# Mixing the dilated groups' outputs on POOL during the next heads' attention, loading the last projection's weights inside the gates, and splitting the norms over two engines

## The chip, the cores and the metric

The program runs on one core of a Trainium2 chip. The metric is the device time of one execution in microseconds (us); times of several runs are given with their median. The engines are called as in the profile: PE (matrix products), DVE (vector), ACT (scalar), POOL (GpSimd) and SP (SyncE, which here issues every DMA, the transposing ones too).

## The reference

A trunk of two layers on 2048 tokens of width 1024. The second layer is the one that the change touches most.

```python
def dilated_mixer(h, w_in):
...
    for g, (window, dil) in enumerate(DIL_GROUPS):      # (128, 1), (512, 4), (2048, 16)
...
        o, lse = dilated_group(q, k, qkv[:, :, 2], window, dil)
        outs.append(o)
        lses.append(lse)
    wts = jax.nn.softmax(jnp.stack(lses, axis=0), axis=0)
    o = jnp.einsum('gbth,gbthd->bthd', wts, jnp.stack(outs, axis=0).astype(jnp.float32))
...
def reference(x, mem, mem_norm_w, norm_w, w_memkv, w_out, w_in_a, ...):
    mem_n = rmsnorm(mem, mem_norm_w)
    for i in range(DEPTH):
        h = rmsnorm(x, norm_w[i])
...
        mem_o = memory_attention(q_mem, mem_n, w_memkv[i])
        branch = jnp.concatenate([mix, mem_o], axis=-1) * jax.nn.silu(gate)
        x = x + branch @ w_out[i]
    return rmsnorm(x, final_norm_w)
```

Layer 0 mixes with gated linear attention (GLA), layer 1 with windowed attention in three groups (six heads of 128 each per group), whose outputs are added with softmax weights. Each layer has four heads of attention into 256 memory tokens (the last 256 of the 1024 branch columns), a SiLU gate and an output projection.

## The kernel before, in words

Tokens go in 16 blocks of 128 or 4 chunks of 512. Products that need more than half precision are made of two half-precision parts and three matmuls (`mm3`, L174-177). The instructions are written in the order of the Python text, and a scheduler then reorders them within each engine by a simulation of its own, keeping dependencies; each engine executes its own stream in order, SP's DMA queue too.

The stages, in the order of time:

- **GLA blocks** (the loop at L605): for each block the projections in four parts (`pre_a` to `pre_d`), `gla1` and `gla2`. Into blocks 7 to 14 the loop also puts the column norms of layer 1's input weights: `norm_of` (L345-351, called at L637-639, four per block, 32 in all) loads a 1 MB tile of weights by `load_raw` and sums the squares of its two halves, both on ACT (L351). The norms are needed to scale the weights before they are split into half-precision parts.
- **A2**, memory attention, gate and output projection of layer 0 by blocks, and the seven operand combinations of a Strassen-like product (`h2s`, stored as `h2_d`; L689-806). Memory attention is `mem_qT`, `mem_sc` (L248-269: scores, maximum L260, its scaling L261, exponentials L265, splitting by `split_P` L165-172) and `mem_pv` (L271-292).
- **The passage** into layer 1: the last operands are transposed, stored and loaded again (L812-822), and `load_ws` (L826) loads the first set of weights, which ACT (L838), DVE (L839) and POOL (L842-848) scale and combine.
- **Products and attention**: `products()` (L1226) yields after each of the seven products of a half (`sw_half`, L854). The main loop (L1247-1256) goes through nine units (three pairs of heads, three groups each), for each of two heads through eight blocks; it calls `advance(to)` (L1242) for product pieces, `att_scores` (L1033), one more piece, and the value products of a block before. The probabilities are split into two parts (ACT L168, POOL L169) and transposed by a DMA (L170) into `pt`, which the value products read. The outputs go to `o_d`, the softmax statistics to `st_d`.
- **Gates** (L1271-1311): `gate_prep` (L1137) makes from the statistics of a pair the factors of the three groups and stores them in `f_d`. `gate_half` (L1161) computes a gate by `silu` (DVE L299, ACT L301-303, DVE L307) and hands each 128 x 512 tile to `gate_item` (L1170): for each of three groups it loads factors (`fb`, a row broadcast to 128 partitions) and outputs (`og`), multiplies (POOL L1182 and L1186, DVE L1189), adds (DVE L1191), multiplies by the gate (DVE L1194) and stores to `br_d`. `mem_item` (L1197) does the same for memory attention's output. The loop at L1307 interleaves the stages of layer 1's memory attention, 19 steps of four, with 56 pieces of the gates.
- **Last projection** (L1316-1377): after all gates, four 1 MB loads of `w_out` (L1344), each split into a high part on ACT (L1345) and a low part on DVE (L1346), then 16 blocks: load branch and residual (`load_b`, L1325), split, products, RMSNorm, store.

Of the kernel before, what the change touches and what calls it, by code (L numbers as in the profile page):

```python
# [7 lines left out]
F32 = mybir.dt.float32  # L8
# [26 lines left out]
def trunk(ctx, tc, a, out):  # L35
# [211 lines left out]
    def mem_sc(mem, qmT, wk, tg, hls, wp3=None):  # L247
# [3 lines left out]
        ps = []  # L251
        for hh in range(2):
            s = bank(ps_g)
# [7 lines left out]
            V.tensor_scalar(out=m2, in0=m2, scalar1=nsc, scalar2=LSP, op0=ALU.mult, op1=ALU.add)  # L261
            p_ = tl(wp3 or wk, [P, 512], F32, tg[1 + hh])
            for jj in range(2):
                j = hh * 2 + jj
                A.activation(out=p_[:, jj * 256:(jj + 1) * 256], in_=s[:, jj * 256:(jj + 1) * 256],  # L265
                             func=AF.Exp, scale=sc, bias=m2[:, jj:jj + 1], accum_out=den[:, j:j + 1])
# [4 lines left out]
    def mem_pv(mem, sd, om, po):  # L271
# [16 lines left out]
        V.tensor_scalar(out=den, in0=den, scalar1=ov, scalar2=None, op0=ALU.mult)  # L288
# [31 lines left out]
    st_d = [tl(dram, [2, 3, T], F32, f"std{h}") for h in range(6)]  # L320
    f_d = [tl(dram, [4, 3, 512], F32, f"fd{h}") for h in range(6)]
# [14 lines left out]
    def load_raw(idx, spool):  # L336
        raw = tl(spool, [P, KT, 256], F32, "stg")
# [7 lines left out]
    def norm_of(idx, spool, junkp):  # L345
        raw = load_raw(idx, spool)
        for j in range(2):
            jv = tl(junkp, [P, D], BF16, "e").rearrange("p (k n) -> p k n", k=KT)
            rv = raw[:, :, j * P:(j + 1) * P]
            acc = nrm[:, 2 * idx + j:2 * idx + j + 1]  # L350
            A.activation(out=jv, in_=rv, func=AF.Square, accum_out=acc)  # L351
# [26 lines left out]
    with ExitStack() as c1:  # L378
# [226 lines left out]
        for b in range(NB):  # L605
            S = gla2(b, pres[b][1], aqs[b], S)
            if b + 2 < NB:
                hT = ga(b + 2)
            if b + 2 < NB:
                pres[b + 2] = pre_a(b + 2, hT)  # L610
            if b + 2 < NB:
                pre_b(*pres[b + 2])
            if b + 2 < NB:
                pre_c(*pres[b + 2])
            if b + 2 < NB:
                pre_d(*pres[b + 2])
            if b + 1 < NB:
# [19 lines left out]
            if 7 <= b < 15:  # L637
                for j in range(4):
                    norm_of((b - 7) * 4 + j, (stg, sga)[j % 2], k2)

    ch = ctx.enter_context(ExitStack())
    h2p = ch.enter_context(pool("h2p", 1, "right"))
    wo_p = ch.enter_context(pool("wo", 1, "right"))
# [4 lines left out]
    with ExitStack() as c2:  # L648
# [138 lines left out]
        for j in range(4):  # L787
            wt = tl(wo_p, [P, 2, KT, 256], F16, f"wo{j}")
# [648 lines left out]
```

## Time and profile before

| | us |
|---|---|
| runs, median of 3 (lowest to highest) | 2884.04 (2874.2 to 2885.29) |
| the profiled execution | 2881.88 |
| its span | 2880.0 |
| PE busy (share of the span) | 2524.7 (88%) |
| DVE | 1655.0 (57%) |
| ACT | 1363.5 (47%) |
| POOL | 844.2 (29%) |

The mean granted PE clock is 0.948. A line such as L1191 is a line of the kernel; an arrow in a name goes from the output tile to the inputs. A group's row gives count, busy us, mean ns of one, and the idle time in front of it with what ended it. A row of waits gives engine, line, what was waited for, total us, times and the longest. The stages lie, in us from the span's start: GLA blocks with norms 280 to 440, A2 500 to 955, the passage 955 to 1001, products and attention 1001 to 2335, gates 2335 to 2658, the passage to the last projection 2658 to 2692, the last projection to 2880.

### The profile page before, as it was taken

To read this page: it belongs to the slowest core of one execution; us is meant where nothing else is said; L and a number is where in the kernel's file an instruction comes from. 1 tells how busy PE (TensorE), PEld (TensorE's weight loads), DVE (VectorE), ACT (ScalarE), POOL (GpSimd) and SP (SyncE) were. 2 spreads that over 40 slices of the span, in tenths; PEclk is the share of its full clock that TensorE was granted. 3 is DMA by queue.
4 is the path that set the end of the run, shared out by engine and by line. 5 is a ranking of instruction groups with operands and counts; after the bars stand their busy time and mean duration, and the time that the engine had idled before them with its cause. 6 is when DMAs were issued, how large, how long until landed. Compare 5 with 4: busy or idle time off the path is not lost. (4 is left out here: it accounts for less than half of the span.)

```text
span 2880.0 us, 54886 instructions
## 1 busy us (share of the span) xinstructions
PE 2524.7 (88%) x21264; PEld 1887.1 (66%) x21264; DVE 1655.0 (57%) x3205; ACT 1363.5 (47%) x3033; POOL 844.2 (29%) x709
## 2 busy tenths in 40 slices
PE   7999789999999398999999999999899986665699
PEld 6888679888888364757575747575757743322487
DVE  6445334666666346566656565657465678876433
ACT  6355864644444144555544455545454544542322
POOL 0000000021112134444444444435344445642000
PEclk9999999999999799999999999999999997777799
DMA  6243873466476835677666667666667768987533
GB/s 203 78 137 115 269 218 103 124 138 152 111 156 139 229 114 148 181 168 181 162 167 167 174 162 177 163 167 174 160 165 178 167 170 187 205 190 187 173 133 123
DMA packets 800747, 469.21 MB, mean 163 GB/s; under 512 B 508466, under 2 KB 745700, under 8 KB 799332
## 3 DMA queue, kind: packets, MB, share of 16 engines
q1 hardware_dynamic: 800484, 465.69, 61.7%
q8 instruction: 167, 2.74, 0.4%
q14 instruction: 96, 0.79, 0.1%
HBM read 274.15 MB, written 130.47 MB: 140 GB/s over the span
## 5 line engine op out<-in xcount | busy, mean ns | idle before, releaser
L175 PE MATMUL ps_mm<-w,hT 128*128 128x256 f16 (+1 forms) x1408 | 392.8, 279 | 16.2 <-ACT v L515 7.2
L176 PE MATMUL ps_mm<-w,hT 128*128 128x256 f16 (+1 forms) x1408 | 391.6, 279 | 0.0
L177 PE MATMUL ps_mm<-w,hT 128*128 128x256 f16 (+1 forms) x1408 | 390.7, 279 | 0.4 <-DVE hT L407 0.4
L176 PEld LDWEIGHTS <-w 128*128 128x128 f16 x2032 | 210.7, 104 | 206.4 <-issue 93.4
L839 DVE SCALAR_TENSOR_TENSOR w<-stg,wsc,w 128x512 f16<-128x512 f32 x224 | 209.7, 937 | 189.3 <-ACT w L838 188.0
L177 PEld LDWEIGHTS <-w 128*128 128x128 f16 x2032 | 210.7, 104 | 148.0 <-issue 19.4
L175 PEld LDWEIGHTS <-w 128*128 128x128 f16 x2032 | 210.5, 104 | 131.2 <-issue 16.5
L838 ACT ACTIVATE w<-stg,wsc 128x512 f16<-128x512 f32 x224 | 160.1, 717 | 213.5 <-DMA stg<-in_w_in_b 72.4
L169 POOL TENSOR_TENSOR ph<-pm,ph 128x512 f16<-128x512 f32 (+2 forms) x144 | 144.3, 1003 | 310.0 <-ACT ph L168 226.2
L1076 ACT ACTIVATE pm<-pm,st,qsc 128x256 f32<-128x256 f32 (+1 forms) x288 | 156.9, 545 | 149.5 <-DVE st L1070 148.6
L169 POOL TENSOR_TENSOR stg<-mp,stg 128x512 f16<-128x512 f32 x16 | 18.5, 1157 | 711.3 <-DMA ogd<-og 503.1
L175 PE MATMUL ps_mm<-w,w 128*128 128x128 f16 (+1 forms) x740 | 189.0, 285 | 16.0 <-DVE cx L880 11.5
L945 DVE SCALAR_TENSOR_TENSOR hl<-cx,hl 128x512 f16<-128x512 f32 x162 | 140.8, 870 | 106.3 <-ACT hl L944 105.5
L177 PE MATMUL ps_mm<-w,w 128*128 128x128 f16 (+1 forms) x740 | 188.3, 284 | 0.0
L176 PE MATMUL ps_mm<-w,w 128*128 128x128 f16 (+1 forms) x740 | 188.2, 284 | 0.0
L944 ACT ACTIVATE hl<-cx 128x512 f16<-128x512 f32 x162 | 100.8, 623 | 167.7 <-DVE cx L880 151.7
L176 PEld LDWEIGHTS <-hT 128*128 128x128 f16 x1408 | 140.6, 100 | 38.7 <-issue 18.7
L175 PEld LDWEIGHTS <-hT 128*128 128x128 f16 x1408 | 141.3, 100 | 21.8 <-issue 1.5
L177 PEld LDWEIGHTS <-hT 128*128 128x128 f16 x1408 | 140.6, 100 | 20.1 <-DVE hT L407 0.7
L897 POOL TENSOR_TENSOR u<-u,p 128x512 f32<-128x512 f32 x64 | 90.0, 1406 | 88.3 <-ACT u L875 88.3
L175 PE MATMUL ps_o<-pt,v 128*128 128x128 f16 (+1 forms) x384 | 77.3, 231 | 43.4 <-DMA pt<-ph 42.8
L175 PEld LDWEIGHTS <-h 128*128 128x128 f16 x800 | 88.2, 110 | 39.1 <-issue 36.9
(402 smaller groups left out, 7975.4 us busy)
## 6 DMA issues: line engine op xcount, KB each, us to landing
stg<-in_w_in_b SPq DMA_DIRECT2D x144, 256.0 KB
stg<-in_w_in_b SPq DMA_DIRECT2D x56, 512.0 KB
qkd<-hl SPq DMA_DIRECT2D x144, 192.0 KB
rope<-in_rope SPq DMA_DIRECT2D x36, 512.0 KB
vud<-hl SPq DMA_DIRECT2D x72, 256.0 KB
q<-qkd SPq DMA_DIRECT2D x72, 256.0 KB
od<-osb SPq DMA_DIRECT2D x72, 256.0 KB
og<-od SPq DMA_DIRECT2D x72, 256.0 KB
```

The source lines that it names most:

```text
L169: G.tensor_tensor(out=lo, in0=src, in1=hi, op=ALU.subtract)
L175: PE.matmul(o, sh, mh, start=first, stop=False, skip_group_check=free)
L176: PE.matmul(o, sh, ml, start=False, stop=False, skip_group_check=free)
L177: PE.matmul(o, sl, mh, start=False, stop=last, skip_group_check=free)
L838: A.activation(out=t[:, 0], in_=src, func=AF.Copy, scale=s1)
L839: V.scalar_tensor_tensor(out=t[:, 1], in0=src, scalar=s1, in1=t[:, 0], op0=ALU.mult, op1=ALU.subtract)
L897: G.tensor_tensor(out=u3, in0=u3, in1=p1, op=ALU.add)
L944: A.activation(out=hi, in_=src, func=AF.Copy, scale=SQ)
L945: V.scalar_tensor_tensor(out=lo, in0=src, scalar=SQ, in1=hi, op0=ALU.mult, op1=ALU.subtract)
L1076: A.activation(out=p_, in_=p_, func=AF.Exp, scale=sc, bias=st[:, sj[jj]:sj[jj] + 1], accum_out=st[:, 16 + sj[jj]:17 + sj[jj]])
```

## The change

1. `norm_step` replaces `norm_of`: each call squares the tile that was loaded two calls earlier, in place, one half on ACT and the other on DVE (`tensor_tensor_reduce`), then loads the next. Four calls stand between the parts of each block from block 7.
2. The first weights of layer 1 are loaded in A2's last step, and the second half's operands after the second set's load.
3. `mem_sc` scales the maxima of both halves in one operation. In layer 1 `mem_pv` leaves out the scaling by the values' factor, and `mem_turn`'s copy on ACT takes it over.
4. `gate_item` is gone. `combos` mixes the groups' outputs of a pair of heads: loads as before, multiplications and one addition on POOL, the last multiplication and addition on DVE, and a store to `acc_d`. It is a generator; `tick`, called for each product piece, steps it. Pair 0 runs from unit 3, pair 1 from unit 6, pair 2 from the start of the gates.
5. Between a block's scores and the value products, two product pieces instead of one.
6. `gate_half` loads the mixed output (`oc`), the first step goes to DVE for one tile of four and to POOL for three, the gate times `oc` to POOL.
7. The order of the memory stages in a step, and of the last gate's halves, is another.
8. The last projection's weights are loaded and split by `out_w` between the last pieces of the gates, and so is the first block's `load_b`; the blocks begin with chunk 0. The low parts of the second half are two tiles of 256 columns, so its products with them are two (120 more matmuls).

```diff
+    def norm_step(spool):
+        if spool in raws:
+            idx, raw = raws.pop(spool)
+            acc = nrm[:, 2 * idx:2 * idx + 2]
+            rv = raw[:, :, 0:P]
+            A.activation(out=rv, in_=rv, func=AF.Square, accum_out=acc[:, 0:1])
+            rv = raw[:, :, P:2 * P]
+            V.tensor_tensor_reduce(out=rv, in0=rv, in1=rv, scale=1.0, scalar=0.0, op0=ALU.mult, op1=ALU.add,
+                                   accum_out=acc[:, 1:2])
+        if left:
+            idx = left.pop(0)
+            raws[spool] = idx, load_raw(idx, spool)
...
+            if n == NB - 1:
+                raw0 = load_raw(0, wp, "w")
...
+    def combos(hp, pl, lag):
+        yield from gate_prep(hp, pl)
+        for hf in range(2):
+            for c, i in ((hf, 0), (hf + 2, 1), (hf + 2, 0), (hf, 1)):
+                h = hp * 2 + i
+                acc = None
+                for g in (2, 1, 0):
+                    fb = tl(pl[0], [P, 16, 32], F32, "fb")
...
+                    og = tl(pl[1], [P, 512], F32, "fo")
...
+                    yield lag[0]
+                    if g == 2:
+                        G.tensor_tensor(out=fb, in0=og.rearrange("p (q l) -> p q l", q=16), in1=fb, op=ALU.mult)
+                    elif g == 1:
+                        f1v = fb.rearrange("p (r f) l -> p r f l", f=4)
+                        G.tensor_tensor(out=f1v, in0=og.rearrange("p (f l r) -> p r f l", f=4, r=4), in1=f1v,
+                                        op=ALU.mult)
+                        G.tensor_tensor(out=fb, in0=fb, in1=acc, op=ALU.add)
+                    else:
+                        ov = og.rearrange("p (l q) -> p l q", q=16)
+                        V.tensor_tensor(out=ov, in0=ov, in1=fb.rearrange("p q l -> p l q"), op=ALU.mult)
+                        V.tensor_tensor(out=ov, in0=ov, in1=acc.rearrange("p q l -> p l q"), op=ALU.add)
+                        SY.dma_start(acc_d[h][c], og)
+                    acc = fb
+                    yield lag[1]
...
         def fin(src, ci, ni, ps):
-            sg = tl(gt, [P, 512], F32, "sg")
-            silu(src, 512, [inv], [neg], sg, ge)
-            post(sg, hf + 2 * ci, ni)
+            c = hf + 2 * ci
+            oc = tl(gb, [P, 512], F32, "oc")
+            SY.dma_start(oc, src_of(c, ni))
+            e = tl(ge, [P, 512], F32, "e")
+            (V if ps else G).tensor_scalar(out=e, in0=src, scalar1=neg, scalar2=87.0, op0=ALU.mult, op1=ALU.min)
+            A.activation(out=e, in_=e, func=AF.Exp)
+            A.activation(out=e, in_=e, func=AF.Ln, bias=one1)
+            A.activation(out=e, in_=e, func=AF.Exp, scale=-1.0)
+            G.tensor_tensor(out=e, in0=e, in1=oc, op=ALU.mult)
+            V.scalar_tensor_tensor(out=e, in0=src, scalar=inv, in1=e, op0=ALU.mult, op1=ALU.mult)
+            SY.dma_start(br_d[c][:, :, row + ni, :], e.rearrange("p (n t) -> p n t", n=4))
...
             for n in range(8):
+                if un in (3, 6) and i == 0 and n == 2:
+                    aux[0] = combos(un // 3 - 1, (cf, cg), (2, 1))
                 advance(28 + LEAD + 42 * un + ((42 if un < 8 else 24) * (i * 8 + n)) // 16)
                 att_scores(H, n, pend)
                 if len(pend) > 1:
-                    advance(done[0] + 1)
+                    advance(done[0] + 2)
                     pend.pop(0)()
...
     for t_ in range(19):
-        for k in (3, 2, 1, 0):
+        for n, k in enumerate((1, 3, 0, 2)):
             mem_stage(k, t_ - k)
-            advance((42 * (4 * t_ + 4 - k)) // 76)
+            advance((42 * (4 * t_ + n + 1)) // 76)
+    advance(49)
+    ch.close()
...
+    porder = [0, 1, 2, 3, 8, 9, 10, 11, 4, 5, 6, 7, 12, 13, 14, 15]
+    out_w(0)
+    out_w(1)
+    advance(51)
+    out_w(2)
+    advance(53)
+    out_w(3)
+    nxt = load_b(porder[0], wp)
     advance(10 ** 6)
```

`cf` holds two buffers, `cg` one; in the gates `gb` and `ge` hold three, `gf` two.

How the streams change, at three places. First ACT at the passage into layer 1. Before, behind the last operand combinations (L760, `stg`) come the puts of the first set's weights (L838, `w<-stg`):

```order
L760 ACTIVATE stg_11390<-t_1643_11392 128x512
L760 ACTIVATE stg_11390<-x_11277 128x512
L760 ACTIVATE stg_11390<-x_11144 128x512
L838 ACTIVATE w_11484<-stg_11481,wsc_5437 128x512
L838 ACTIVATE w_11489<-stg_11481,wsc_5437 128x512
L838 ACTIVATE w_11493<-stg_11481,wsc_5437 128x512
```

After, at the same place (the lines are now L778, L853 and L859; `w_11185` is the tile loaded early, `stg_11430` the second set's):

```order
L778 ACTIVATE stg_11322<-t_1586_11324 128x512
L778 ACTIVATE stg_11322<-x_11209 128x512
L778 ACTIVATE stg_11322<-x_11073 128x512
L853 ACTIVATE stg_11430<-stg_11430,wrat_5384 128x8x128
L859 ACTIVATE w_11405<-w_11185,wsc_5382 128x512
L859 ACTIVATE w_11410<-w_11185,wsc_5382 128x512
```

The scaling of the second set's tile has moved ahead of the first set's puts.

Second, SP in a unit of attention. Before, transposes (`pt`), stores and loads of queries, keys and values alternate:

```order
L990 DMA qkd_1_96_184<-hl_20548 192x1x512
L1022 DMA q_20677<-qkd_0_93_181 128x8x128
L1022 DMA k_20678<-qkd_1_94_182 128x8x128
L1025 DMA v_20482<-vud_0_121_209 128x8x128
L1110 DMA od_1_45_133<-osb_20529 128x512
L170 DMA_TRANSPOSE pt_20567<-ph_20566 128x8x128
L990 DMA qkd_0_95_183<-hl_20586 192x1x512
```

After, in a unit with `combos` (L1193 loads factors, L1197 and L1199 a group's outputs, L1212 stores the sum):

```order
L1193 DMA fb_20390<-fd_68_156 128x512
L1212 DMA accd_63_151<-fo_20289 128x512
L170 DMA_TRANSPOSE pt_19965<-ph_19964 128x8x128
L976 DMA vud_1_128_216<-hl_20020 128x1024
L1193 DMA fb_20491<-fd_68_156 128x512
L976 DMA vud_0_127_215<-hl_20074 128x1024
L1199 DMA fo_20392<-od_2_40_128 128x16x32
L976 DMA vud_1_128_216<-hl_20158 128x1024
L170 DMA_TRANSPOSE pt_20104<-ph_20103 128x8x128
```

The transposes now stand behind loads and stores of the combinations, of which `fo` has one buffer.

Third, SP at the end of the gates. Before, the loads of `w_out` (L1344) and of the first block (L1327) stand near and behind the last stores of the gates (`brd`):

```order
L1344 DMA raw_4463_32243<-in_w_out 128x8x256
L1352 DMA fw_32253<-in_final_norm_w 128x1024
L1201 DMA brd_150_238<-sg_32049 512x1x128
L1199 DMA og_32151<-omTd_144_232 128x512
L1201 DMA brd_149_237<-sg_32103 512x1x128
L1199 DMA og_32176<-omTd_143_231 128x512
L1201 DMA brd_151_239<-sg_32144 512x1x128
L1199 DMA og_32201<-omTd_140_228 128x512
L1201 DMA brd_151_239<-sg_32169 512x1x128
L1327 DMA w_32247<-brd_150_238 128x1024
```

After (L1371 loads `w_out`, L1381 and L1382 a block, L1231 and L1239 are the gates' load and store):

```order
L1231 DMA oc_32118<-omTd_152_240 128x512
L1371 DMA raw_32093<-in_w_out 128x8x256
L1239 DMA brd_157_245<-e_31971 512x1x128
L1231 DMA oc_32142<-omTd_151_239 128x512
L1239 DMA brd_155_243<-e_31995 512x1x128
L1382 DMA w_32097<-x1d_125 128x1024
L1381 DMA w_32097<-brd_155_243 128x1024
L1231 DMA oc_32166<-omTd_148_236 128x512
L1239 DMA brd_156_244<-e_32069 512x1x128
L1239 DMA brd_158_246<-e_32120 512x1x128
```

The last weight load stands before the gates' last five stores, and so does the first block's load.

More of the change, by code (lines that the diff above doesn't have):

```diff
@@ L251, in mem_sc @@
         ps = []
+        sb = [bank(ps_g) for hh in range(2)]
         for hh in range(2):
-            s = bank(ps_g)
+            s = sb[hh]
             for jj in range(2):
@@ L260, in mem_sc @@
             V.tensor_reduce(out=m2, in_=s.rearrange("p (a b) -> p a b", a=2), axis=AX.X, op=ALU.max)
-            V.tensor_scalar(out=m2, in0=m2, scalar1=nsc, scalar2=LSP, op0=ALU.mult, op1=ALU.add)
+        V.tensor_scalar(out=mx, in0=mx, scalar1=nsc, scalar2=LSP, op0=ALU.mult, op1=ALU.add)
+        for hh in range(2):
+            s = sb[hh]
             p_ = tl(wp3 or wk, [P, 512], F32, tg[1 + hh])
@@ L320, in trunk @@
     st_d = [tl(dram, [2, 3, T], F32, f"std{h}") for h in range(6)]
+    acc_d = [tl(dram, [4, P, 512], F32, f"accd{h}") for h in range(6)]
     f_d = [tl(dram, [4, 3, 512], F32, f"fd{h}") for h in range(6)]
@@ L334, in trunk, with load_raw @@
     nrm = tl(cp, [P, 2 * (NJ + NQ)], F32, "nrm")
-    def load_raw(idx, spool):
-        raw = tl(spool, [P, KT, 256], F32, "stg")
+    def load_raw(idx, spool, tag="stg"):
+        raw = tl(spool, [P, KT, 256], F32, tag)
         for c0, ap in wcols[idx]:
@@ L343, in load_raw @@
         return raw
[L345 to L351, printed above, removed]
+    raws = {}
+    def norm_step(spool):
[10 more added lines that the diff above has]
+            raws[spool] = idx, load_raw(idx, spool)
+    left = list(range(NJ + NQ))
     kv_d = tl(dram, [2, 4, P, 512], F16, "kvd")
@@ L1162, in gate_half, with tick @@
+    aux = [None, 0]
+    def tick():
+        aux[1] -= 1
+        while aux[0] is not None and aux[1] <= 0:
+            aux[1] = next(aux[0], None)
+            if aux[1] is None:
+                aux[0], aux[1] = None, 0
+    def gate_half(ops, idx, hf, src_of, row):
         inv, neg = winv[:, idx:idx + 1], wneg[:, idx:idx + 1]
         def fin(src, ci, ni, ps):
-            sg = tl(gt, [P, 512], F32, "sg")
-            silu(src, 512, [inv], [neg], sg, ge)
-            post(sg, hf + 2 * ci, ni)
@@ L1307, in trunk, with out_w @@
     for t_ in range(19):
-        for k in (3, 2, 1, 0):
+        for n, k in enumerate((1, 3, 0, 2)):
             mem_stage(k, t_ - k)
-            advance((42 * (4 * t_ + 4 - k)) // 76)
+            advance((42 * (4 * t_ + n + 1)) // 76)
+    advance(49)
+    ch.close()
+    f0 = ctx.enter_context(pool("f0", 1, "right"))
+    WSH = [P, KT, 256]
+    wo2 = []
+    def out_w(j):
+        if j % 2 == 0:
+            wl = tl(f0, [P, KT, 512], F32R, "wl0") if j == 0 else None
+            wo2.append((tl(f0, [P, KT, 512], F32R, f"wh{j}"),
+                        [wl[:, :, i * 256:(i + 1) * 256] for i in range(2)] if j == 0 else [], wl))
+        wh, wl, _ = wo2[-1]
+        if j >= 2:
+            wl.append(tl(wp, WSH, F32R, "w"))
+        raw = tl((stg, f0)[j % 2], WSH, F32, ("stg", "raw")[j % 2])
+        hi, lo = wh[:, :, j % 2 * 256:j % 2 * 256 + 256], wl[j % 2]
+        SY.dma_start(raw, a["w_out"][1, :, j * 256:(j + 1) * 256].rearrange("(k p) n -> p k n", p=P))
+        A.activation(out=hi, in_=raw, func=AF.Copy)
+        V.tensor_tensor(out=lo, in0=raw, in1=hi.bitcast(F32), op=ALU.subtract)
```

186 lines of the change are left out of this document (80 added, 106 removed).

## The prediction

> **What bounds the kernel now.** I read the windows first, cut where the program changes stage, then the waits inside each window, the groups of instructions of the gates, and last the chain of waits around the start of the output projection. The windows (columns: window, us, then busy us and instructions of PE, PE weight loads, DVE, ACT and POOL, the granted PE clock, the DMA share, GB/s), in order: the GLA blocks with the column norms, the passage into the dilated layer, products with dilated attention, gates, the passage to the last projection, the last projection.
>
> ```profile
> 280.00:440.00 160.00, 131.66 (x1006) 113.86 (x1006) 53.63 (x120) 117.43 (x277) 0.00 (x0) 0.93 0.79 237
> ...
> 955.00:1001.00 46.00, 8.22 (x73) 6.99 (x73) 10.45 (x12) 5.91 (x11) 6.19 (x4) 0.64 0.91 244
> 1001.00:2335.00 1334.00, 1249.58 (x11851) 856.99 (x11851) 796.67 (x1591) 650.50 (x1415) 599.04 (x522) 0.98 0.66 167
> 2335.00:2658.00 323.00, 211.97 (x1079) 103.92 (x1078) 252.49 (x372) 138.10 (x313) 155.99 (x103) 0.80 0.80 187
> 2658.00:2692.00 34.00, 0.70 (x4) 0.10 (x1) 18.52 (x20) 17.97 (x20) 0.00 (x0) 0.55 0.77 244
> 2692.00:2880.00 188.00, 181.69 (x792) 147.24 (x792) 65.08 (x82) 45.76 (x114) 0.00 (x0) 0.98 0.37 130
> ```
>
> PE is busy 94% of the attention's 1334 us and 97% of the last 188. The time without PE lies in four places: 28 us in the norms' window, 38 in the passage, 84 in attention, and 111 + 33 in the gates and the passage behind them. In the gates DVE is the fullest engine, 252.49 of 323 us, 0.78; PE runs at a clock of 0.80. The waits there (engine line, who is waited for, total us, times, longest):
>
> ```profile
> ACT e L301 <- DVE e L299: 95.3, 26, 8.0
> ...
> POOL fb L1182 <- DMA fb<-fd: 66.1, 16, 7.2
> DVE sg L307 <- DMA brd<-sg: 41.2, 17, 5.6
> ...
> PE ps_mm L175 <- DVE cx L880: 28.2, 7, 9.6
> PE ps_o L283 <- DMA mp<-mh: 25.6, 10, 5.2
> ```
>
> ACT waits for DVE to come round to a gate's first step; PE's longest wait is for a DVE addition; POOL waits for loads that DVE's queue frees late. So the gates go at DVE's pace.
>
> **Norms.** The squares (a group: busy us, mean ns) wait for weights:
>
> ```profile
> L351 ACT ACTIVATE e<-stg 128x1024 bf16<-128x1024 f32 x64 | 67.4, 1054 | 37.3 <-DMA stg<-in_w_in_b 34.9 <-ACT e L351 0.9 <-ACT la L482 0.5
> ```
> ```profile
> ACT e L351 <- DMA stg<-in_w_in_b: 28.3, 21, 8.7
> ```
>
> 32 of 64 go to DVE, 32 x 1.05 = 34 us off ACT; on DVE a 128x1024 pass is not shown in this form, and at the same 1.05 the 53.63 us become 87 of 160, with room. What stays are the 32 MB of loads at 237 GB/s and a DMA share of 0.79. The new step consumes a load two steps old, so some of the 28.3 us goes, but the loads are pressed into the same blocks. PE is idle 28 us: I take -8; ends -25 (the whole wait) and +5 (the same loads with DVE's squares ahead of the scan's work).
>
> **A2 and the passage.** One small operation fewer per stage lies under PE work: 0. In the passage ACT waits 19.3 us:
>
> ```profile
> 980.58 0.63 ACT L760 ACTIVATE stg<-x 128x512 f16<-128x512 f32 x1 [1.04 <-POOL x L781]
> 1000.49 0.72 ACT L838 ACTIVATE w<-stg,wsc 128x512 f16<-128x512 f32 x1 [19.28 <-DMA tq<-stg]
> ```
>
> The weights come earlier now, but what ends the wait is the last transposes, and set 1's scaling, with its own load, now stands ahead of set 0's puts on ACT. I take 0; ends -12 and +6.
>
> **Attention.** PE's largest wait here, and SyncE's (its queue holds the transposes):
>
> ```profile
> PE ps_o L175 <- DMA pt<-ph: 42.8, 37, 3.2
> ```
> ```profile
> SPq L170 <- POOL xr L987: 65.2, 39, 3.1
> ```
> ```profile
> L987 POOL COPY xr<-cx 32x512 f32<-32x512 f32 x108 | 72.2, 669 | 71.6 <-DVE cx L880 63.0 <-ACT pm L1076 2.7 <-DMA std<-stT 1.4
> ```
> ```profile
> og<-od SPq DMA_DIRECT2D x72, 256.0 KB
> ```
>
> One more product piece between scores and values covers some of the 42.8 us. Against it stand the combinations of two pairs: 16 items of 3 steps, 7 transfers of 256 KB each, 29.4 MB, which at the gates' full rate (187 / 0.80 = 234 GB/s) are 125 us of DMA in two stretches of about 238 us (74 of the stage's some 414 product pieces each); the share there goes from 0.66 to 0.92. They add 112 issues to SyncE, and 48 POOL and 32 DVE operations. Each load of a group's output waits for POOL or DVE to have used the one buffer, and queued behind it on SyncE are the transposes that PE's value products wait for. Attention's POOL, 599 us of 1334, gets 72 more (rows below); so no engine is full, and what counts is the order on SyncE. I take -12: 25 off the 42.8, 13 given back. Ends: -35 (nearly all of it) and +48 (1 us for each of 48 steps).
>
> **Gates.** The groups of POOL, then of DVE, in the gates (count, busy us, mean ns):
>
> ```profile
> L169 POOL TENSOR_TENSOR mh<-mp,mh 128x512 f16<-128x512 f32 x32 | 47.5, 1490 | 30.6 <-ACT mh L168 28.8 <-DMA fb<-fd 1.6
> L1186 POOL TENSOR_TENSOR fb<-og,fb 128x512 f32<-128x512 f32 x24 | 38.2, 1590 | 28.1 <-DMA fb<-fd 16.4 <-DMA og<-od 8.2 <-DVE om L290 2.8
> L1182 POOL TENSOR_TENSOR fb<-og,fb 128x512 f32<-128x512 f32 x24 | 34.7, 1444 | 78.2 <-DMA fb<-fd 66.1 <-DVE sg L1194 5.3 <-DVE om L292 4.3
> ```
> ```profile
> L1191 DVE TENSOR_TENSOR fb<-fb,fb 128x512 f32<-128x512 f32 x48 | 43.5, 906 | 6.9 <-POOL fb L1186 6.5
> L1194 DVE TENSOR_TENSOR sg<-fb,sg 128x512 f32<-128x512 f32 x24 | 27.8, 1158 | 0.4
> L1189 DVE TENSOR_TENSOR fb<-og,fb 128x512 f32<-128x512 f32 x24 | 26.2, 1090 | 1.9 <-DMA og<-od 1.8
> ...
> L261 DVE TENSOR_SCALAR mmx<-mmx,cols 128x2 f32<-128x2 f32 x32 | 17.3, 547 | 0.1
> ...
> L299 DVE TENSOR_SCALAR e<-cx,wneg 128x512 f32<-128x512 f32 x24 | 14.9, 623 | 0.2
> L288 DVE TENSOR_SCALAR mden<-mden,cols 128x4 f32<-128x4 f32 x16 | 12.0, 753 | 0.1
> ...
> L1200 DVE TENSOR_TENSOR sg<-og,sg 128x512 f32<-128x512 f32 x8 | 5.5, 690 | 0.2
> ```
>
> DVE loses 43.5 + 27.8 + 26.2 + 14.9 + 12.0 + 5.5, and half of the score scaling, about 9 (32 of 0.55 us become 16): 139. It gets pair 2's 8 items of two operations, 8 x (1.09 + 0.91) = 16. Its 271 us of both windows become 148. POOL loses 38.2 + 34.7. It gets 32 products of a gate at 1.49 (the nearest two-input row), 47.7; 8 items of 1.44 + 1.59 + 1.49, 36.2; and 24 minima with one input, which no row shows at this size: between 0.67 (the 32x512 copy above) and 1.59, I take 1.2, 28.8. 156.0 - 72.9 + 112.7 = 196. The 152 loads of 256 KB in the gates (72 outputs, 72 factors, 8 of memory) become 80, with 8 stores more, and the new orders of the memory stages and of the last gate's halves lie under that: 0. So POOL becomes the fullest, before PE: 212 us at 0.80, about 170 at full clock. An engine that leads here is at work 0.8 of the time, as DVE was: 196 / 0.8 = 245 us. Bounds: 0.67 and 1.59 for the minima are 183 and 205 us of POOL, 229 and 257; at a share of 0.95 with the former, 193, so PE with 205 decides.
>
> The passage to the last projection, in the chain of waits (start us, us, step):
>
> ```profile
> 2658.74 0.39 SPq L1344
> 2659.17 8.52 DMA raw<-in_w_out
> ...
> 2686.78 4.08 DMA w<-brd
> 2690.96 1.06 ACT w L1331
> 2692.07 0.80 PE ps_x L175
> ```
>
> The four weight loads and their splits now lie in the last quarter of the gates, and the first block's operands come from chunk 0, stored before. What is late next is the last product's bank and the second half's low weights, some 6 us by the last two rows. Gates from 2335 take 245 + 6: the projection starts at 2586, not 2692, -106. By the bounds -147 (205 + 5) to -68 (283 + 6, below).
>
> **Last projection.** 120 more products of half the width, the same columns: 0. A start at half clock: without the idle 34 us, -3.
>
> Sum: -8 + 0 + 0 - 12 - 106 - 3 = -129 against the profiled 2881.88, so 2753; the median of the runs is 2.2 above that execution: **2755 us**.
>
> **Rivals.**
> *POOL is dearer.* If its two-input operations with one operand fresh from a load take twice DVE's 1090, 2.18 us, the gate's products are 69.8, the items 8 x (2 x 2.18 + 2 x 0.91) = 49.4 with an addition at twice 0.91: POOL 231, gates 289 us, total 2799. Against it: the same multiplication takes 1444 on POOL, 1.3 times. Chance 0.12. The Trainium skill, GPSIMD Engine Reference, section Engine selection, advises against this move: elementwise work with two inputs is about two times slower there than on VectorE. By that rule the sum is this rival's; the trace's 1444 against 1090 agrees only in direction.
>
> *Attention pays.* The 48 steps hold SyncE for 1 us each before a transpose, and the earlier piece gains nothing: -117 + 48 = -69, 2815. For it: SyncE's 65.2 us of waits for POOL, which the new operations lengthen. POOL's times also depend on who runs beside it, the row of the gates above against the same subtraction in A2:
>
> ```profile
> L169 POOL TENSOR_TENSOR stg<-mp,stg 128x512 f16<-128x512 f32 x16 | 18.5, 1157 | 711.3 <-DMA ogd<-og 503.1
> ```
>
> 1490 beside a busy DVE, 1157 here. Against it: two pieces now cover the step. Chance 0.14. The Trainium skill, SBUF — State Buffer, section Who interferes with whom, says that DVE with two inputs in SBUF and GpSimd's reads exclude each other. By this rule the gates' POOL would get cheaper when DVE's 104 such operations go, and attention's dearer; the 0.33 us of difference agrees in direction.
>
> *Slower.* The same queue at a higher price: a group's load waits for POOL's step, that for an earlier load, and every transpose behind it on SyncE is late by both. At 2.7 us for each of the 48 steps, all on PE, -117 becomes +13, slower by 0.5%; at 3.5 us it is +51, 2935. For it: three operations of 1.5 us make 4.5 us an item; against it, 94% of PE is busy there with pieces that need no transpose. Chance 0.07.
>
> *Better.* POOL near 0.95, PE decides the gates at nearly full clock, 170 / 0.83 = 205 us: 2715. Chance 0.08.
>
> *The gain doesn't come.* Gates keep their 323 us because the chain through ACT, POOL and DVE of one gate with three buffers sets the pace, as ACT's 95.3 us of waiting could also be read; only the passage's 34 shrinks by some 14: 2870. Against it: DVE at 0.78. Chance 0.05.
>
> **How the numbers follow.** The forecast keeps 0.54, with a range of its own of 2715 to 2795. A measurement of this kernel can tell about 0.5%, 14 us, from no change. Forecast, dearer POOL, paying attention and the better case are faster: 0.88; the gain that doesn't come is within: 0.05; slower 0.07. The range 2700 to 2825 takes in all but the last two of these and the forecast's tails.
>
> **What would show it.** Right: gates of about 250 us with POOL at 0.8 and DVE near 0.6; no 34 us gap before the projection; the attention stretch within 15 us of 1334 less 12; the wait for pt near 20 to 30 us. Wrong: an attention stretch over 1360 us with SyncE waiting at the new loads; POOL over 230 us in the gates; a gap before the last projection that stays.

## The result

The changed kernel takes 2893.23 us (median of 11 runs, 2887.72 to 2906.56), the kernel before 2878.76 us in 11 runs; the ratio is 1.0051, with a 95% interval of 1.0034 to 1.0068. It is slower, by half a per cent, where 4.5% less was forecast. The profiled execution has a span of 2891.5 us.

The windows of the changed kernel, cut at the same events as before (columns as in the prediction): norms, A2 to the last store of x1, the passage, products and attention, gates up to the first product of the last projection, the rest.

```profile
280.00:440.00 160.00, 140.11 (x1083) 121.54 (x1082) 88.60 (x187) 85.13 (x209) 0.00 (x0) 0.93 0.75 229
500.00:973.00 473.00, 431.27 (x3982) 377.14 (x3979) 284.53 (x597) 212.92 (x463) 79.63 (x60) 0.97 0.57 135
973.00:1022.00 49.00, 12.76 (x185) 12.70 (x186) 13.76 (x14) 12.11 (x20) 13.02 (x9) 0.62 0.86 265
1022.00:2429.00 1407.00, 1260.54 (x11701) 858.25 (x11699) 838.97 (x1642) 640.13 (x1405) 668.45 (x568) 0.97 0.72 176
2429.00:2702.00 273.00, 188.55 (x1049) 96.75 (x1047) 154.41 (x217) 149.51 (x326) 197.53 (x131) 0.83 0.74 186
2702.00:2890.00 188.00, 182.79 (x912) 153.51 (x912) 67.51 (x85) 49.71 (x119) 4.63 (x3) 0.98 0.38 136
```

In the kernel before, the same events lie at 965, 1014, 2331 and 2692 us. A2 ends 8 us later (the last x1 store is issued at 972.9, not 964.6), the passage takes 49 us in both, attention 1407 instead of 1317 (+90), gates and the passage behind them 273 instead of 361 (-88), the rest is 1.5 us longer. The gain in the gates is there, and attention gives all of it back.

The loss has a place. Counted by the last store of each unit's outputs, units 1, 2, 5 and 8 take 502 us in the changed kernel and 506 before; units 3, 4, 6 and 7, in which `combos` runs, take 667 and 572 (the 569 in the first expectation below is a slip). The waits over the whole attention, PE's two largest and three of SyncE's, of which the last two are at the new loads:

```profile
PE ps_o L175 <- DMA pt<-ph: 86.1, 41, 5.7
PE ps_g L175 <- DVE mx L1087: 25.0, 21, 4.6
```
```profile
SPq L170 <- POOL ph L169: 68.1, 46, 3.6
...
SPq L1193 <- DMA fb<-fd: 17.3, 9, 3.9
...
SPq L1199 <- DMA accd<-fo: 12.6, 7, 3.3
```

The wait for the transposed probabilities (`pt`) has doubled from 42.8 us. SyncE's waits at the transposes for POOL have not grown: in units 1 to 8 the one for the subtraction L169 is 62.5 us here and 73.4 in the kernel without mixing (e1 below). What is new are its waits at the lines of the mixing, 89 us there in all. The prediction had named both parts of this as a sign of being wrong: attention over 1360 us, and SyncE waiting at the new loads. The units 1 to 8 as one window, first before, then changed:

```profile
1253.40:2331.00 1077.60, 1009.71 (x9652) 697.41 (x9651) 656.50 (x1347) 534.36 (x1190) 485.42 (x429) 0.99 0.68 170
```
```profile
1259.20:2428.80 1169.60, 1039.28 (x9683) 713.06 (x9682) 706.97 (x1403) 532.11 (x1190) 563.27 (x479) 0.96 0.76 182
```

No engine but PE is near full: PE 1039 of 1170, POOL 563, DMA share 0.76. PE's busy time has grown by 30 us at nearly the same count, beside a granted clock of 0.96 instead of 0.99, and its idle time from 68 to 130 us.

These windows are the measure of the experiments below, since single times of different chips differ by some us. How well they repeat is seen where the attention is the same: 1169.6, 1169.8 and 1172.4 us in the changed kernel, e8 and e12; 1067.2, 1067.7, 1068.3 and 1072.7 us without mixing and with two pieces in e1, e4, e20 and e21. So a difference of 5 us or less in one run tells nothing.

### The profile page after: what moved, and what is told of

The parts are those of the page before. It is cut to its first block, busy times and chain, and to the rows that moved or that the text cites. A ratio compares the mean times of both kernels' runs of the same rounds, so it can differ in the third digit from the quotient of the medians.

```text
span 2891.5 us, 55208 instructions
## 1 busy us (share of the span) xinstructions
PE 2526.5 (87%) x21384; PEld 1897.8 (66%) x21384; DVE 1621.2 (56%) x3141; ACT 1326.7 (46%) x2969; POOL 967.1 (33%) x789
## 5 line engine op out<-in xcount | busy, mean ns | idle before, releaser
L860 DVE SCALAR_TENSOR_TENSOR w<-stg,wsc,w 128x512 f16<-128x512 f32 x217 | 199.6, 920 | 160.6 <-ACT w L859 159.7
L169 POOL TENSOR_TENSOR stg<-mp,stg 128x512 f16<-128x512 f32 x16 | 18.9, 1180 | 724.4 <-ACT stg L168 724.4
L859 ACT ACTIVATE w<-stg,wsc 128x512 f16<-128x512 f32 x217 | 155.2, 716 | 201.7 <-DMA stg<-in_w_in_b 85.1
L169 POOL TENSOR_TENSOR ph<-pm,ph 128x512 f16<-128x512 f32 (+2 forms) x144 | 149.6, 1040 | 210.4 <-ACT ph L168 122.6
L175 PE MATMUL ps_mm<-w,w 128*128 128x128 f16 (+1 forms) x744 | 186.4, 280 | 8.9 <-DVE cx L901 8.7
L176 PE MATMUL ps_mm<-w,w 128*128 128x128 f16 (+1 forms) x744 | 186.3, 280 | 0.0
L177 PE MATMUL ps_mm<-w,w 128*128 128x128 f16 (+1 forms) x744 | 186.0, 279 | 0.0
```

Source lines behind the costliest of these rows:

```text
L169: G.tensor_tensor(out=lo, in0=src, in1=hi, op=ALU.subtract)
L175: PE.matmul(o, sh, mh, start=first, stop=False, skip_group_check=free)
L176: PE.matmul(o, sh, ml, start=False, stop=False, skip_group_check=free)
L177: PE.matmul(o, sl, mh, start=False, stop=last, skip_group_check=free)
L859: A.activation(out=t[:, 0], in_=src, func=AF.Copy, scale=s1)
L860: V.scalar_tensor_tensor(out=t[:, 1], in0=src, scalar=s1, in1=t[:, 0], op0=ALU.mult, op1=ALU.subtract)
```

## The experiments

The runs are to tell apart three theories of the loss: *in-order engines* (SyncE, POOL and DVE hold the chain of the transposes while one waits for another), *bandwidth* (the bytes fill the DMA), and *POOL's work* (its operations alone). The diffs show the lines that matter, against the changed kernel (those of e16 and e20 against e15). Line numbers in a row are those of that run's own kernel. "Before" in brackets is the kernel before, run beside it on the same chip. The runs e1, e2, e3, e6, e7, e17 and e21 leave out parts of the mixing and so compute something else than the reference.

**Without mixing (e1).**

```diff
-                if un in (3, 6) and i == 0 and n == 2:
-                    aux[0] = combos(un // 3 - 1, (cf, cg), (2, 1))
...
```

> Leaves out the mixing of pairs 0 and 1 altogether (factors, loads, arithmetic, store); their gates read one group's stored output instead, so the gates do the same work. If the mixing is what lengthens attention, units 3, 4, 6 and 7 (667 us together in the changed kernel, 569 before) come back to 565 to 580 and the time falls by about 90 us, to 2795 to 2815. If it is the second product piece between scores and values, or another edit, they stay above 620 and the time stays above 2850.

2792.48 us (before: 2879.5). Units 3, 4, 6 and 7 take 570 us.

```profile
1259.30:2326.50 1067.20, 1012.86 (x9685) 701.22 (x9683) 653.97 (x1347) 531.84 (x1188) 495.88 (x431) 0.99 0.71 171
```

So the mixing of two pairs costs 1169.6 - 1067.2 = 102 us in attention, 2.1 us for each of 48 steps, and 97 of them lie in units 3, 4, 6 and 7. With neither attention nor gates having to do it, the kernel is 87 us faster than before. Of the 102, 26 are PE's own busy time, beside a clock of 0.96 instead of 0.99, and 76 are time in which PE is idle.

**Loads alone (e2).**

```diff
-                    if g == 2:
+                    if not calc:
+                        pass
+                    elif g == 2:
```

> Keeps the factors, the loads and the store of pairs 0 and 1 and leaves out the multiplications and additions on POOL and DVE. Theory of bandwidth: the four units stay about 650 us, loss of 80 or more of the 98. Theory of in-order engines (SyncE's queue and POOL each hold the transposes' chain while they wait for the other): without readers neither waits for long, loss 15 to 40. Theory of POOL's work alone: loss under 15.

2869.73 us (before: 2879.5).

```profile
1256.40:2396.20 1139.80, 1031.48 (x9685) 706.57 (x9683) 669.33 (x1371) 531.06 (x1190) 491.90 (x431) 0.97 0.77 186
```

1139.8, 73 of the 102 us, 64 of them in units 3, 4, 6 and 7 (634 us): less than bandwidth alone should cost, more than the in-order theory allowed for loads that nobody reads. The loads stand where they stood, from 1545 and 1997 us (1547 and 2009 in the changed kernel), but are through sooner.

**Arithmetic alone (e3).**

```diff
-                    fb = tl(pl[0], [P, 16, 32], F32, "fb")
+                    fb, og = fix[g % 2], fix[2]
```

> Keeps the 48 POOL and 32 DVE operations of pairs 0 and 1, on three tiles that are written once, and leaves out the factors, the loads and the store. Theory of POOL's work alone: the four units stay about 650 us, loss of 80 or more. Theory of in-order engines: the operations never wait for a load, loss 15 to 40, and this loss with that of the loads alone is well under 98. Theory of bandwidth: loss under 15.

2837.99 us. It doesn't tell: with nothing to wait for, the scheduler put the operations into unit 0, which ends at 1289.1 instead of 1259.3 us, and units 1 to 8 are without mixing (1072.5 us).

**All mixing in the gates (e4).**

```diff
+    for _ in combos(0, (gf, gf), (1, 0)):
+        pass
...
+        yield from combos(1, (gf, gf), (0, 1))
+        yield from combos(2, (gf, gf), (0, 1))
```

> All three pairs are mixed in the gates, pair 0 ahead of the first piece, the rest two steps per piece; everything else as in the changed kernel. Attention falls by about 90 us as without mixing. In the gates POOL gets 72 us more, about 270 in all: at 0.8 busy 340 us instead of 273 from the first gate to the last projection, time 2870. If the gates are not paced by POOL but by another chain, they grow by less than 30 us and the time is under 2835.

3040.28 us: from the last unit to the last projection 519.5 us.

```profile
2330.10:2849.60 519.50, 232.39 (x1050) 108.58 (x1048) 194.51 (x274) 155.93 (x329) 250.35 (x180) 0.68 0.60 155
```

POOL has 250 us of work in it, half the time, DMA 0.60. So POOL's load doesn't set the pace; my price of 340 us was far off. That a chain of single steps through two buffers does is my reading, not shown: the longest waits of DVE and ACT there are for POOL (139 and 95 us), those of POOL for the factors' loads (91).

**Short transfers, with the operations (e6) and without (e7).**

```diff
-        yield from gate_prep(hp, pl)
+    def combos(hp, pl, lag, fix=None):
+        if not fix:
+            yield from gate_prep(hp, pl)
...
+                        fb, og = fix[g % 2], fix[2]
+                        SY.dma_start(fb[:, 0, 0:8], o_d[h][0][:, c * 512:c * 512 + 8])
+                        SY.dma_start(og[:, 0:8], o_d[h][g][:, c * 512:c * 512 + 8])
...
```

> The 112 transfers of pairs 0 and 1 are kept in number and place but carry 8 of 512 columns, and the 48 POOL and 32 DVE operations stay at full size (with other operators, since their operands are not the real ones; the factors are left out). Without mixing the time was 2792, with loads alone 2870, with all 2893. Theory of bandwidth: what stays is the operations and the issues, 2805 to 2825. Theory of in-order engines (SyncE held by issues and waits, POOL by waits for loads): the order and the waits are the same, 2850 to 2890.

> As the run with loads alone (2870), but the 112 transfers carry 8 of 512 columns; no operations, no factors; the gates of pairs 0 and 1 read another stored output. Theory of bandwidth: the 77 us of the loads go with the bytes, 2792 to 2805. Theory of the queue: issuing and waiting on SyncE costs the same for a short transfer, 2835 to 2870.

2846.68 and 2834.42 us (before: 2873.0). The windows of e6, then of e7:

```profile
1257.40:2381.60 1124.20, 1030.51 (x9684) 707.21 (x9683) 706.74 (x1379) 531.89 (x1188) 568.26 (x479) 0.97 0.68 163
```
```profile
1258.80:2367.70 1108.90, 1020.65 (x9678) 701.35 (x9677) 654.83 (x1343) 530.60 (x1186) 496.39 (x431) 0.97 0.68 165
```

e6 is 57 us longer than without mixing, e7 42. But the transfers did not keep their place. Without the factors the loads depend on the stored outputs alone, and the scheduler put them as soon as these are there: in e7 from 1135 us on, in unit 0, instead of from 1547, and pair 0's last sum is stored at 1559 us instead of 1807. By units:

| us | e1 | e2 | e6 | e7 | changed |
|---|---|---|---|---|---|
| units 3, 4, 6, 7 | 570 | 634 | 596 | 569 | 667 |
| units 1, 2, 5, 8 | 497 | 506 | 529 | 540 | 502 |

The 42 us of e7 lie in units 1, 2 and 5, and none of them where the changed kernel loses. So the two runs give no price of the issues where the mixing has them, and 42 can't be taken from 73 to get that of the bytes. They show one thing: 112 transfers of a 64th of the bytes can cost 42 us, at a DMA share of 0.68 as before, so a loss needs neither many bytes nor POOL's operations. SyncE waits 79 us at their lines in e7, most of it for an earlier transfer into or out of the same tiles. What stands of the parts is e2's: 73 us for factors, loads and stores without the operations, 29 more with them (102 - 73); no theory holds alone.

**More pieces per step (e9).**

```diff
-                    aux[0] = combos(un // 3 - 1, (cf, cg), (2, 1))
+                    aux[0] = combos(un // 3 - 1, (cf, cg), (3, 2) if un == 3 else (3, 1))
```

> The mixing of pair 0 is spread over 5 product pieces per step instead of 3, of pair 1 over 4. The same bytes and operations over a longer stretch. If the loss comes from the DMA share being close to full in the two stretches (0.81 and 0.78 against 0.69), it falls with the share: 2860 to 2878. If each step costs what it costs, wherever it stands (queue, operations), the time stays at 2885 to 2900.

2895.89 us. It doesn't tell either: the stores of the mixed tiles are issued at nearly the same times as in the changed kernel (the first at 1579 and 1580 us, the eighth at 1798 and 1807), because the scheduler follows the buffers and not the place in the text. Whether thinner mixing would cost less wasn't tried.

**Another queue: ACT (e10), POOL (e11).**

```diff
-    def combos(hp, pl, lag):
+    def combos(hp, pl, lag, qe=SY):
...
-                        SY.dma_start(acc_d[h][c], og)
+                        qe.dma_start(acc_d[h][c], og)
...
-                    aux[0] = combos(un // 3 - 1, (cf, cg), (2, 1))
+                    aux[0] = combos(un // 3 - 1, (cf, cg), (2, 1), A)
```

In e11 the last argument is `G`, POOL's queue.

> All transfers of the mixing of pairs 0 and 1 are issued from ACT's queue instead of SyncE's; nothing else. The run with short transfers alone lost 42 us against none, which I put on SyncE's queue. If that is so, those 40 or so come back: attention 60 us longer than without mixing instead of 102, time 2840 to 2860. If bytes and operations make the loss and SyncE has nothing to do with it, 2885 to 2900. If ACT is held by loads that wait for the one buffer, over 2900.

> The same with POOL's queue, where a load stands behind the operations that free its buffer anyway. Theory of SyncE's queue: 2840 to 2870, if issuing on POOL is short. If POOL pays more for an issue than SyncE does (112 issues, no row of the runs shows it), its operations are late and the time stays at 2885 or above.

2894.64 and 2876.04 us (before: 2873.96). Units 1 to 8, ACT's queue, then POOL's:

```profile
1260.60:2416.50 1155.90, 1037.74 (x9684) 708.30 (x9683) 714.90 (x1403) 531.65 (x1190) 565.88 (x479) 0.97 0.76 184
```
```profile
1252.80:2407.10 1154.30, 1029.22 (x9685) 703.98 (x9683) 727.27 (x1404) 533.22 (x1190) 636.62 (x592) 0.97 0.77 184
```

14 and 15 us come back, not 40 (and with ACT's queue the gates are 11 us longer, 284, so that the time doesn't show it). On POOL three of the groups that issue, mean ns of one:

```profile
L1199 POOL DMA_DIRECT2D fo<-od x32 | 32.1, 1003 | 14.0 <-DMA accd<-fo 10.4 <-POOL fb L1202 1.5 <-ACT pm L1097 1.2
...
L1193 POOL DMA_DIRECT2D fb<-fd x48 | 26.6, 555 | 28.8 <-DVE fo L1210 17.6 <-DMA qkd<-hl 9.7 <-DVE st L1091 1.2
...
L1197 POOL DMA_DIRECT2D fo<-od x16 | 9.4, 590 | 0.0
```

An issue takes POOL 0.6 to 1.0 us, 77 us with the stores, and it stands there behind the wait for its buffer too. The traces also tell how late SyncE issues a transpose after POOL has made its input (from the end of L169 to the start of L170, mean of the 64 in units 3, 4, 6 and 7): 0.33 us without mixing, 1.61 in the changed kernel, 2.47 with loads alone, 0.73 with ACT's queue and 1.77 with POOL's. So ACT's queue takes most of the lateness away and gives 14 of 102 us back, and with the loads alone the lateness is larger and the loss smaller. SyncE's order is a part of the loss, then, and not the whole. That it is no part can't be said either: ACT and POOL make the transposes' input, and the issues hold them instead. How bytes, issues and waits for the buffers share in the loss stays open.

**One product piece (e14), and without mixing (e17).**

```diff
-                    advance(done[0] + 2)
+                    advance(done[0] + 1)
```

> The changed kernel with one product piece between a block's scores and its values, as before. The wait for pt is 86 us in the changed kernel and 34 without mixing, 43 before. If the second piece hides part of the transposes that the mixing delays, the wait grows to 100 to 130 us and the time to 2905 to 2935. If it does nothing, 2888 to 2898.

> No mixing of pairs 0 and 1 and one product piece. With two pieces this was 2792 and the wait for pt 34 us. If the second piece hides transposes, 2797 to 2812 and the wait near 43 as before; if it costs by itself as it does beside the mixing, 2778 to 2788.

2878.38 us with mixing (before: 2873.96), 2801.29 without (before: 2881.57). Units 1 to 8, with and without:

```profile
1257.90:2416.40 1158.50, 1022.13 (x9644) 697.86 (x9643) 701.76 (x1402) 534.67 (x1192) 565.20 (x477) 0.98 0.76 183
```
```profile
1263.60:2335.30 1071.70, 1007.17 (x9654) 695.04 (x9653) 656.96 (x1347) 534.37 (x1190) 485.24 (x429) 0.99 0.69 171
```

Without mixing the second piece gains 4.5 us at most (1071.7 to 1067.2), no more than the windows of one kernel differ; beside it, it costs 11 (1158.5 to 1169.6), against both of my expectations there. With one piece the mixing costs 87 us.

**POOL's queue and one piece (e19)**, the two edits above together.

> The changed kernel with the mixing's transfers on POOL's queue (2876) and one piece (2878). If the two add up: 2857 to 2866. If both take away the same delay of the transposes: 2870 to 2880.

2872.26 us (before: 2881.57), units 1 to 8 in 1146.5 us. The time lies in the second range, but the ranges compared times of two chips on which the kernel before differs by 7.6 us. In attention the two gain 15.3 and 11.1 us against the changed kernel, 26 together, and this run 23: most of it adds up. Against the kernel before on its own chip it is 9 us faster, in a single run.

**The old scores (e8), the late first weights (e12).**

```diff
-        sb = [bank(ps_g) for hh in range(2)]
...
-            s = sb[hh]
+            s = bank(ps_g)
```
```diff
-                raw0 = load_raw(0, wp, "w")
+                raw0 = None
```

> The changed kernel with the old form of the memory scores (each half's maximum scaled by itself, one bank at a time). The layer 0 output blocks end 8 us later in the changed kernel than before, and 6 to 12 us later in each variant. If the two banks held together are the reason, the last of the x1 stores comes at 963 to 967 and the time at 2880 to 2888; the gates may grow by 3 to 9 us from 16 more small DVE operations. If another edit is the reason, the store stays at 970 to 977.

> The changed kernel without the early load of the first weights of layer 1 (they are loaded where they were before). In the changed kernel this load stands on SyncE ahead of four transposes and waits for PE to free its buffer; the output block before the last comes 10 us later there. If that load is the reason, the last x1 store comes at 962 to 967 instead of 973, and the attention begins 5 to 9 us earlier: 2884 to 2889. If not, the store stays at 970 or later and the time at 2890 to 2896.

e8 2885.97 us (before: 2873.0), the last x1 store at 968.5, between the two cases: A2 takes 415.0 us from the first to the last x1 store, 413.8 in the changed kernel, 405.1 before; the scores aren't the reason. e12 2910.09 us (before: 2873.96), beyond both ranges: the last store comes at 975.1, and unit 0 ends at 1270.0 instead of 1259.2. So the early load isn't the reason either; it gains some 9 us in the passage, by this one run. What makes A2 8 us longer stays open.

**Mixing in the gates as before (e15), and its last product on POOL (e16).** Below the lines of the gate's product in each; e15 puts back all of `gate_item`, and with it the gate's first step on DVE, the old numbers of buffers in the gates and one product piece in attention.

```diff
+        sv = sg.rearrange("p (l q) -> p q l", q=16)
+        V.tensor_tensor(out=sv, in0=acc, in1=sv, op=ALU.mult)
```
```diff
-        V.tensor_tensor(out=sv, in0=acc, in1=sv, op=ALU.mult)
+        G.tensor_tensor(out=sv, in0=acc, in1=sv, op=ALU.mult)
```

> The mixing is back in the gates as before (per tile, adds and the gate's product on DVE), one product piece in attention; norms, scores, early weights and the early loads of the last projection stay as changed. Theory: of the 88 us that the gates and the passage behind them gained, only the passage's 28 (34 less 6) belong to the early weights, the other 60 to the moved mixing, which costs 102 in attention: 2845 to 2862. If the early loads delay a DVE-bound gates stage by what they save, 2870 to 2885. If most of the gates' gain came from the other small edits there, under 2835.

> As the run before, and the product of the gate and the mixed output (24 of 1.16 us on DVE) on POOL. DVE falls to about 215 us in the gates, POOL rises to about 192. If the gates go at DVE's pace with 0.78 busy, they fall by 25 to 35 us against the run before: 2815 to 2835. If POOL's extra work stands in the same chain, no gain: within 8 us of the run before.

e15 takes 2873.64 us, ratio to before 0.9957 (0.9939 to 0.9976): faster than the kernel before by 0.4%, and than the changed one, whose ratio is 1.0051. That is the second range, though the early loads do save something. e16 takes 2889.17, ratio 1.0018 (1.0004 to 1.0033). The gates of e15, then e16:

```profile
2335.60:2679.20 343.60, 214.72 (x1091) 102.80 (x1089) 245.80 (x352) 153.18 (x328) 151.83 (x104) 0.80 0.83 197
```
```profile
2333.40:2692.20 358.80, 215.58 (x1091) 104.44 (x1089) 224.99 (x328) 153.79 (x328) 183.37 (x128) 0.79 0.78 189
```

The early weights, with the small edits beside them, take the gates from 361 to 344 us, not by 28 but by 17 (by 11 in e20 below, with the same gates), and the last projection is 3 to 5 us longer in both, so that 8 to 12 are left at the end. The moved mixing, with the other edits of the gates that e15 puts back, takes them from 344 to 273. And taking 21 us off DVE and putting 32 on POOL made the stage 15 us longer: DVE, with 0.78 busy, did not set the pace in the way that I had read it. Which chain did is not shown.

**Two pieces on e15 (e20).**

```diff
-                    advance(done[0] + 1)
+                    advance(done[0] + 2)
```

> The mixing in the gates as before, everything else as changed, with two product pieces between scores and values. If the second piece gains what it did without mixing (2801 to 2792), 9 us on 2874: 2860 to 2868, ratio to before 0.992 to 0.995. If it costs here too, 2876 or above.

2870.61 us (before: 2877.45), ratio 0.9973 (0.9956 to 0.9990): faster than the kernel before, and no better than e15.

**The minima on DVE, without mixing (e21).**

```diff
-            (V if ps else G).tensor_scalar(out=e, in0=src, scalar1=neg, scalar2=87.0, op0=ALU.mult, op1=ALU.min)
+            V.tensor_scalar(out=e, in0=src, scalar1=neg, scalar2=87.0, op0=ALU.mult, op1=ALU.min)
```

> No mixing of pairs 0 and 1 (2792), and all 32 minima of the gates on DVE: POOL falls from 197 to about 150 us there, DVE rises from 154 to about 170. If POOL sets the gates' pace, the 273 us fall by 25 or more, to a time of 2755 to 2770. If the pace is set by the memory attention's chain of split, transpose and value product, by less than 10: 2782 to 2795.

2778.11 us (before: 2884.92). The gates without mixing, with the minima on POOL (e1) and on DVE:

```profile
2326.50:2600.30 273.80, 186.52 (x1050) 95.21 (x1048) 154.36 (x218) 150.10 (x326) 197.09 (x131) 0.83 0.73 186
```
```profile
2335.00:2588.10 253.10, 181.53 (x1051) 93.03 (x1049) 169.49 (x243) 149.92 (x330) 152.71 (x109) 0.87 0.78 202
```

44 us less on POOL are worth 21 us: POOL's share in the pace is real, though not all of it.

## Why the prediction was wrong

**Attention is the step that failed**: "so no engine is full, and what counts is the order on SyncE. I take -12: 25 off the 42.8, 13 given back". The 25 were 5 at most (e17 against e1), and beside the mixing the second piece costs 11. The 13 given back were 102 with two pieces and 87 with one; the high end of +48, 1 us for each of 48 steps, was too low as well: a step costs 2.1. The prediction had seen the place, had counted the right things (112 issues, 72 us of POOL), and had the DMA share too high, 0.92 where 0.81 and 0.78 came. But it took "no engine is full" for cheap, and PE is full there, at the 94% that it had itself read: what delays PE's operands has little to hide behind. Without mixing PE is idle for 54 us of units 1 to 8, with it for 130, and its own products take 26 us more. As for "what counts is the order on SyncE": the transposes do go out later behind the new loads, 1.61 us after their input instead of 0.33, but with the issues off that queue only 14 to 15 of the 102 us come back (e10, e11). The loads without their operations cost 73, the operations 29 more; how the 73 divide stays open.

**The rival that ends slower** was this one at a different price: it needed 2.7 us a step because the other terms were put at -117. They came to -79 (8 - 88 + 1.5), so 1.6 us a step, 79 in all, was the point of no gain, and attention grew by 90.

**Gates: -106 forecast, -88 measured.** The loads of the engines were right, POOL put at 196 us and at 197.5, DVE at 148 and at 154; the rule that the fullest engine leads and is at work 0.8 of the time was not. Three groups of POOL there:

```profile
L1233 POOL TENSOR_SCALAR e<-cx,wneg 128x512 f32<-128x512 f32 x23 | 47.3, 2060 | 6.9 <-DMA brd<-e 3.8 <-DVE cx L901 3.1
L1237 POOL TENSOR_TENSOR e<-e,oc 128x512 f32<-128x512 f32 x30 | 45.8, 1532 | 20.1 <-ACT e L1236 12.5 <-DMA oc<-accd 7.6
L169 POOL TENSOR_TENSOR mh<-mp,mh 128x512 f16<-128x512 f32 x32 | 40.9, 1290 | 17.3 <-ACT mh L168 17.3
```

The sum of POOL held by luck, because errors met. The minima take 2.06 us and not 1.2, outside the bounds of 0.67 to 1.59 that I took from a copy and a product (47 us instead of 29); the subtraction takes 1.29 instead of 1.49 (41 instead of 47), and the rest of POOL's work is some 10 us less than put. The Trainium skill's rule on DVE and GpSimd excluding each other (SBUF — State Buffer, section Who interferes with whom) would make it cheaper, since 88 of DVE's operations with two inputs have left; the direction agrees, but in e15, where the old mixing is back in the gates, the subtraction takes 1.35, so at most 0.06 of the 0.20 us go with these operations, and the cause isn't shown. The product at 1.53 is as forecast, far from the 2.18 of the rival with a dearer POOL. POOL's share is 0.72 instead of 0.8, and 44 us less on it are worth 21 (e21), at a share of 0.60; in e16 the stage grew while the fullest engine, DVE, lost 21 us. That e21's gates take 253 us, near the 251 that were forecast, is luck.

**The gap before the last projection** shrank to 12 us, where 6 were forecast. The first product of the last projection, before and then changed, with PE's idle time in front of it:

```profile
2692.07 0.80 PE L175 MATMUL ps_x<-wh,w 128*128 128x512 f32 x1 [33.36 <-ACT w L1331]
```
```profile
2702.04 0.79 PE L1420 MATMUL ps_x<-wh,w 128*128 128x512 f32 x1 [11.71 <-ACT w L1385]
```

It waits for the first block's load and its split on ACT, as before. The four weight loads no longer stand in between, but they have not left the chain: it now goes through one of them and its splits ahead of the gates' last tiles.

```profile
2674.20 5.41 DMA raw<-in_w_out
2679.63 1.92 ACT wh L1372
...
2687.45 2.28 DVE w L1373
```

By e15 and e20 this edit and the small ones beside it are worth 11 to 17 us instead of 28; the loads and splits take some of it back inside the gates, as this chain suggests; how much, no run shows by itself.

**Norms: -8 forecast, 0 measured.** The first x1 store is issued at 559.1 us, 559.5 before. Both engines now wait for the same loads:

```profile
DVE stg L359 <- DMA stg<-in_w_in_b: 38.2, 21, 4.5
ACT stg L357 <- DMA stg<-in_w_in_b: 37.7, 23, 4.1
```

PE is busy 140 us of that window instead of 132, but the stage as a whole doesn't end earlier.

**A2 and the passage: 0 and 0 forecast, +8 and 0 measured.** The 8 us are unexplained. In the passage the set 1 scaling does stand ahead of set 0's puts, as the order had shown, and the early load still gains 9 us (e12) against loading it late in this order. **Last projection: -3 forecast, +1.5 measured**; no run takes it apart, and in e15 and e20 it is 3 to 5 us longer than before.

**The scale.** The chance of 0.88 for faster rested on terms of which the largest sure one, -106, was to be paid for by one with an unknown price. Moved work was costed at its destination by the engines' load, with a guess of 1 us a step at most for the queue. Two us a step instead of one as the high end (+96), with the gates at their own end of -68, would have made -8 + 96 - 68 - 3 = +17, and the result would have lain inside; that much is known only now.

## What to carry to other kernels

Work that is moved beside a chain of engines that wait for each other is not paid by the room left on the other engines: here some 71 us saved in one stage cost 87 to 102 in another, where PE was at work 94% of the time and every other engine 61% or less. Price such a move per step, with a run that moves the loads alone, before building it, and look in the trace whether the steps stand where they are meant to: the runs that were to price the arithmetic and the short transfers had their work moved by the scheduler. And test the parts of a change apart: here the versions that leave the mixing where it was and take the rest are 0.3 to 0.4% faster than the kernel before, and the whole change is 0.5% slower.

## What the runs showed of the hardware

A multiplication and minimum of one 128x512 f32 tile with two scalars takes 2.06 us on POOL. The same on DVE, in e21:

```profile
L1233 DVE TENSOR_SCALAR e<-cx,wneg 128x512 f32<-128x512 f32 x24 | 18.3, 780 | 5.8 <-DMA brd<-e 5.7
```

POOL multiplies two such tiles in 1.53 us, so on POOL the operation with one tile was the dearer one, and 2.6 times DVE's. The Trainium skill, GPSIMD Engine Reference, section Engine selection, calls operations with one input roughly line-rate there; this row doesn't bear that out for the scalar form. Issuing a 256 KB load took POOL 0.56 to 0.59 us with rows of 2 KB (L1193 and L1197 in e11) and 1.0 us with rows of 128 or 512 bytes (L1199). And with the mixing, PE's busy time in units 1 to 8 is 1.026 times that without it at the same count of products (1039.3 and 1012.9 us), beside a mean granted clock of 0.96 instead of 0.99, though no single wait of PE there was over 7.1 us.
